# Attention scores on half the array: two heads on the partitions, three products of 64 rows per head

## The chip, the cores and the metric

The kernel runs on one core of a Trainium2 chip. The metric is the device time in microseconds of one execution. A profiled execution gives the trace; its span goes from the first to the last instruction, and the execution's own time is a little longer.

## What is computed

One decoder layer on 2048 tokens of width 1024. After a first RMSNorm the input is projected to u (512 columns), q (8 heads of 64), k and v (2 heads of 64 each). u goes through an S5 state-space branch with a GLU at its end; q, k and v go through attention in a sliding window of 128 with a sink per head. Both branches are normalised, joined, projected by w_out and added to the input; a SwiGLU layer follows. The part that the change touches:

```python
def one_block(args):                       # a block is 128 queries
    q_blk, k_blk, v_blk, blk = args        # k_blk, v_blk: the block before and this one, 256 keys
    valid = band & (blk * BLOCK - BLOCK + kj >= 0)
    s = jnp.einsum('bqhgd,bkhd->bhgqk', q_blk, k_blk).astype(jnp.float32) * scale
    s = jnp.where(valid, s, MASK_VALUE)
    m = jnp.maximum(jnp.max(s, axis=-1, keepdims=True), sink)
    p = jnp.exp(s - m)
    p = p / (jnp.sum(p, axis=-1, keepdims=True) + jnp.exp(sink - m))
    return jnp.einsum('bhgqk,bkhd->bqhgd', p.astype(v_blk.dtype), v_blk)
```

A head has 64 dimensions; four query heads share one key head.

## The kernel before

Precision comes from splitting: a float32 operand x is written as hi + lo, both of the type fp32r, which TensorE multiplies in one pass, and a product of two such operands is hi*hi + hi*lo + lo*hi (`mm3`, lines 219 to 221; the splits are lines 170 and 171, ScalarE for hi and VectorE for lo). Plain float32 operands take longer per column; the state-space products (`ps_S`, `ps_Y`), the transposes (`ps_pt`, `ps_oT`) and the attention outputs (`ps_O`) are of that kind.

The layer runs in stages: the projection to u; the projection to q, k, v woven with the state-space branch; the mixing stage; the SwiGLU layer, which takes more than half of the time. The mixing stage (`phase_mix`) weaves two generators. `dense_stream` does, for each of four blocks of 512 tokens, the GLU products (`ps_z`) and then the output projection (`ps_wo`), and `attn_stream` does attention in 16 tiles of 128 queries. `step` pulls the next step of the attention stream at high priority; first come `lead` = 6 steps, and then a number of steps per dense step that a rate sets (`lg`, `rate`). The program is not run in the order of the text: a planner puts each engine's instructions into an order by priority and by when their operands and buffers will be there, and inserts the waits. DMAs that are issued from one queue (SP's, mostly) are issued in order, so one that waits for a buffer holds up those behind it.

`attn_block` prepares a block of 512 tokens. k lies on the partitions twice, rows 0 to 63 and rows 64 to 127 with the same 64 dimensions (two loads, `kraw`), and is split into KH and KL. q is loaded in four pairs of heads, each pair twice as well, into rows 0 to 63 and into rows 64 to 127 (two loads of 256 KB per pair, line 797, buffers `qraw`, two of them, shared with `kraw`). For each head a tile QS of 128 rows is made: a copy to fp32r of all rows (line 800), and then in rows 64 to 127 the remainder (line 801, recorded as line 75, the helper `tt`). So QS holds q's hi in the upper half and q's lo in the lower half. Each of these five preparations ends in a `yield`.

`attn_tile` computes the scores of 128 queries with 256 keys. Per head there are two products over all 128 rows: QS with KH gives (hi + lo) * KH (line 820), and QS with KL adds (hi + lo) * KL (line 821). Two heads share a PSUM bank (`ps_sc`), so a tile fills four banks of eight, out of a group of four that the transposes and outputs of attention use as well (`bank`, tag "pa"). ScalarE copies a bank's first 128 keys to `prob` (line 826), and VectorE writes the second 128 over it where the mask allows (line 827). Maximum, exponential, transposes, outputs and the split of the result follow, each in a step of its own. `mx` and what comes after want all eight heads.

The state-space branch (`ssm_pair`) has the only products of the stage before that use half of the array: `ps_S` (line 658) has a stationary operand of 128 rows and 64 columns, one for each half of the output partitions.

Of the kernel before, what the change touches and what calls it, by code (L numbers as in the profile page):

```python
# [9 lines left out]
F32 = mybir.dt.float32  # L10
F32R = mybir.dt.float32r
# [3 lines left out]
ALU = mybir.AluOpType  # L15
# [4 lines left out]
P = 128  # L20
# [5 lines left out]
TB = SEQ // NB  # L26
# [7 lines left out]
MASKED = -1e30  # L34
# [9 lines left out]
def f32(ap):  # L44
    return ap.bitcast(F32)


class Layer:
# [730 lines left out]
    def attn_block(self, b, ready):  # L779
        nc, aw = self.nc, self.aw  # L780
        KH = aw.tile([P, 2, TB + P], F32R, tag="KH", name=f"KH_{b}")
        KL = aw.tile([P, 2, TB + P], F32R, tag="KL", name=f"KL_{b}")
        if b:
            for new, old in zip((KH, KL), self.kh_prev):
                nc.vector.tensor_copy(new[:, :, 0:P], f32(old[:, :, TB:TB + P]))
        self.kh_prev = (KH, KL)
        kraw = aw.tile([P, 2, TB], F32, tag="qraw", name=f"kraw_{b}", bufs=2)
        for o in (0, 64):
            nc.sync.dma_start(kraw[o:o + 64], self.k_d[b].rearrange("v r t -> r v t"))
        nc.scalar.copy(KH[:, :, P:], kraw)  # L790
        self.tt(KL[:, :, P:], kraw, f32(KH[:, :, P:]), ALU.subtract)
        yield
        QS = []
        for h in range(0, 8, 2):
            raw = aw.tile([P, 2, TB], F32, tag="qraw", name=f"qraw_{b}_{h}", bufs=2)
            for o in (0, 64):
                nc.sync.dma_start(raw[o:o + 64], self.q_d[b][h:h + 2].rearrange("h r t -> r h t"))
            for k in range(2):
                q = aw.tile([P, TB], F32R, tag="QS", name=f"QS_{b}_{h + k}", bufs=8)
                nc.scalar.copy(q, raw[:, k, :])  # L800
                self.tt(q[64:128], raw[64:128, k, :], f32(q[64:128]), ALU.subtract)
                QS.append(q)
            yield
        self.MA[b] = []
        ready[b] = (QS, KH, KL)

    def attn_tile(self, i, QS, KH, KL):

        nc, aw = self.nc, self.aw
        b, t = i // 4, i % 4  # L810
        tq = slice(t * P, (t + 1) * P)
        p = aw.tile([P, 8, P], F32, tag="prob", name=f"prob_{i}")
        for hp in range(4):
            sb = self.bank([P, 2, 2 * P], "sc")
            for h2 in range(2):
                h = hp * 2 + h2
                v = h // 4
                lo = P if i == 0 else 0
                ks = slice(t * P + lo, t * P + 2 * P)
                nc.tensor.matmul(sb[:, h2, lo:], QS[h][:, tq], KH[:, v, ks], start=True, stop=False)  # L820
                nc.tensor.matmul(sb[:, h2, lo:], QS[h][:, tq], KL[:, v, ks], start=False, stop=True)
            ph = p[:, hp * 2:hp * 2 + 2, :]
            if i == 0:
                nc.gpsimd.memset(ph, MASKED)
            else:
                nc.scalar.copy(ph, sb[:, :, 0:P])
            nc.vector.copy_predicated(ph, self.mask_qj.unsqueeze(1).to_broadcast([P, 2, P]), sb[:, :, P:])
        yield
        mx = self.tmp([P, 8], tag="mx")
        nc.vector.tensor_reduce(out=mx, in_=p, axis=AX.X, op=ALU.max)  # L830
        nm = self.tmp([P, 8], tag="nm")
        nc.vector.scalar_tensor_tensor(out=nm, in0=mx, scalar=self.rq[:, i:i + 1], in1=self.sinks,
                                       op0=ALU.mult, op1=ALU.max)
        es = self.tmp([P, 8], tag="es")
        self.tt(es, self.sinks, nm, ALU.subtract)
        nc.scalar.activation(es, es, AF.Exp)
        n = self.o1
        nc.vector.scalar_tensor_tensor(out=p[:, :n], in0=p[:, :n], scalar=self.rq[:, i:i + 1],
                                       in1=nm[:, :n].unsqueeze(2).to_broadcast([P, n, P]),
                                       op0=ALU.mult, op1=ALU.subtract)  # L840
        self.ts(nm[:, n:], nm[:, n:], -1.0, None, ALU.mult, ALU.bypass) if n < 8 else None
        for h in range(n, 8):
            nc.scalar.activation(p[:, h, :], p[:, h, :], AF.Exp, bias=nm[:, h:h + 1], scale=self.rq[:, i:i + 1])
        nc.scalar.activation(p[:, :n], p[:, :n], AF.Exp)
        yield
        if i:
            dv = aw.tile([P, 2, 65], F32, tag="dv", name=f"dv_{i}")
            self.tt(dv, self.V[:, i], self.V[:, i - 1], ALU.subtract, nc.gpsimd)
        else:
            dv = self.V[:, 0]  # L850
        pts = []
        for v in range(2):
            pt = self.bank([P, 4, P], "pt")
            for g in range(4):
                nc.tensor.transpose(pt[:, g, :], p[:, v * 4 + g, :], self.ident)
            pa = None
            if i:
                pa = aw.tile([P, 4, P], F32, tag="pa", name=f"pa_{i}_{v}")
                nc.scalar.copy(pa, pt)
            pc = aw.tile([P, 4, P], F32, tag="pc", name=f"pc_{i}_{v}")  # L860
            self.tt(pc, pa if i and self.o9 else pt, self.mask_jq.unsqueeze(1).to_broadcast([P, 4, P]), ALU.mult,
                    nc.gpsimd if i and self.o9 else None)
            pts.append((pc, pa))
        yield
        o = aw.tile([P, 8, 64], F32, tag="o", name=f"o_{i}")
        for v in range(2):
            O = self.bank([P, 4, 65], "O")
            for g in range(4):
                if i:
                    nc.tensor.matmul(O[:, g, :], pts[v][1][:, g, :], self.V[:, i - 1, v, :], start=True, stop=False)  # L870
                nc.tensor.matmul(O[:, g, :], pts[v][0][:, g, :], dv[:, v, :], start=(i == 0), stop=True)  # L871
            den = self.tmp([P, 4], tag="den")
            hs = slice(v * 4, v * 4 + 4)
            self.tt(den, O[:, :, 64], es[:, hs], ALU.add)
            nc.vector.reciprocal(den, den)
            self.tt(o[:, hs, :], O[:, :, 0:64], den.unsqueeze(2).to_broadcast([P, 4, 64]), ALU.mult)
        jk = aw.tile([P, 8, 64], BF16, tag="ojunk", name=f"ojunk_{i}", bufs=1)
        nc.scalar.activation(jk, o, AF.Square, accum_out=self.ssq_a[:, i:i + 1])
        yield
        oT = self.bank([P, 4, P], "oT")  # L880
        for c in range(4):
            nc.tensor.transpose(oT[:, c, :], o[:, 2 * c:2 * c + 2, :].rearrange("p h d -> p (h d)"), self.ident)
        mh = self.am.tile([P, 4, P], F32R, tag="mah", name=f"mah_{i}")
        ml = self.am.tile([P, 4, P], F32R, tag="mal", name=f"mal_{i}")
        self.split(mh, ml, oT)
        self.MA[b].append((mh, ml))
        yield
# [652 lines left out]
```

## Time and profile before

| | us |
|---|---|
| median of 3 runs | 2167.53 |
| lowest and highest | 2164.43 and 2172.02 |
| profiled execution, its own time | 2164.03 |
| its span | 2162.3 |
| TensorE busy (matmuls) | 2012.2 |
| VectorE busy | 1389.5 |
| ScalarE busy | 925.1 |
| TensorE's granted clock, mean | 0.975 |

In the views below PE is TensorE's matmuls, PEld its weight loads (which run beside the matmuls), DVE VectorE, ACT ScalarE, POOL GpSimd, SPq the DMA queue of SyncE. Times are us from the span's start unless marked ns. Matmuls are pipelined, so the recorded duration of one is longer than the distance to the next; what a matmul costs in a stream is the distance between starts. "128\*128" or "128\*64" is the part of the array in use, rows by columns. PEclk is the granted clock as a share of full speed.

### The profile page before, as it was taken

The page shows a single profiled execution, that of the slowest core. Times are in us where ns is not written, and L with a number is a line of the kernel's source. Part 1 is how long each engine was busy: PE and PEld are TensorE (multiplying, and loading weights), DVE is VectorE, ACT ScalarE, POOL GpSimd, SP SyncE. Part 2 cuts the span into 40 slices and gives each one's busy share as a digit, 9 for nine tenths or more (in the row PEclk, how much of TensorE's full clock was granted, in tenths as well). Part 3 has the DMA queues.
Part 4 walks back from the last instruction along what each step waited for, and adds up shares of the span by engine and source line. Part 5 has one row for each costly group of instructions (what it writes and reads, how often), then busy time and mean ns, then how long its engine had stood idle before and what let it go on. Part 6 is the DMA issues. An engine that isn't in the chain of part 4 may idle for free.

```text
span 2162.3 us, 25813 instructions
## 1 busy us (share of the span) xinstructions
PE 2012.2 (93%) x9200; PEld 1631.6 (75%) x9200; DVE 1389.5 (64%) x2199; ACT 925.1 (43%) x1468; POOL 301.7 (14%) x655
## 2 busy tenths in 40 slices
PE   7998887999999797999989998999999999999996
PEld 5777665787878675878768876887788888888885
DVE  7876888887676748556455655446766555554446
ACT  6433114976566545333323334345333333334443
POOL 3211000112223322212122110001100000000001
PEclk9999998999899998999999999999999999999998
DMA  8566657534246745657666476666523222246665
GB/s 276 213 229 191 200 148 190 144 100 158 67 148 202 270 155 178 240 138 204 208 194 155 153 264 218 199 192 231 171 102 124 95 99 105 89 165 224 204 195 185
DMA packets 177425, 379.73 MB, mean 176 GB/s; under 512 B 32864, under 2 KB 53856, under 8 KB 177104
## 3 DMA queue, kind: packets, MB, share of 16 engines
q1 hardware_dynamic: 138112, 259.89, 38.1%
q0 software_dynamic: 32512, 109.79, 15.6%
q10 hardware_dynamic: 6672, 8.40, 1.3%
q8 instruction: 72, 1.18, 0.2%
q14 instruction: 57, 0.47, 0.1%
HBM read 281.87 MB, written 119.21 MB: 185 GB/s over the span
## 4 chain that ended last, share of the span: by engine, by line
PE 42%; issue 27%; DMA 10%; DVE 7%; POOL 4%; ACT 3%; SPq 0%; DVEq 0%; POOLq 0%; ACTq 0%
PE ps_dn L221 5%; PE ps_dn L219 5%; PE ps_dn L220 5%; PE ps_gb L219 2%; PE ps_gb L221 2%; PE ps_gb L220 2%; PE ps_wo L219 2%; PE ps_wo L221 2%; PE ps_wo L220 2%; DMA hx<-hd 1%; DMA hr<-bTd 1%; DMA tab<-tabd 1%; PE ps_O L871 1%; PE ps_O L870 1%; PE ps_gc L219 1%
## 5 line engine op out<-in xcount | busy, mean ns | idle before, releaser
L219 PE MATMUL ps_gb<-bh,wh 128*128 128x512 f32 x704 | 280.3, 399 | 17.6 <-ACT wh L170 8.3
L221 PE MATMUL ps_gb<-bh,wl 128*128 128x512 f32 x704 | 275.8, 394 | 3.8 <-DVE wl L171 3.7
L220 PE MATMUL ps_gb<-bl,wh 128*128 128x512 f32 x704 | 277.7, 394 | 0.3 <-DVE bl L171 0.2
L221 PE MATMUL ps_dn<-wh_d,wl_x 128*128 128x512 f32 x616 | 241.4, 393 | 7.5 <-DVE wl_x L171 5.5
L219 PE MATMUL ps_dn<-wh_d,wh_x 128*128 128x512 f32 x616 | 241.3, 392 | 6.1 <-ACT wh_x L170 3.2
L220 PE MATMUL ps_dn<-wl_d,wh_x 128*128 128x512 f32 x616 | 240.7, 391 | 0.0
L219 PEld LDWEIGHTS ps_gb<-bh,wh 128*128 128x128 f32 x704 | 133.4, 190 | 54.3 <-ACT wh L170 10.4
L221 PEld LDWEIGHTS ps_gb<-bh,wl 128*128 128x128 f32 x704 | 133.4, 189 | 34.5 <-DVE wl L171 4.9
L220 PEld LDWEIGHTS ps_gb<-bl,wh 128*128 128x128 f32 x704 | 133.5, 190 | 29.8 <-DVE bl L171 1.5
L219 PE MATMUL ps_gc<-bh,wh 128*128 128x512 f32 x352 | 138.6, 396 | 6.9 <-ACT bh L170 6.7
L221 PEld LDWEIGHTS ps_dn<-wh_d,wl_x 128*128 128x128 f32 x616 | 115.8, 189 | 36.3 <-DVE wl_x L171 9.2
L170 ACT CAST wh<-fr 128x1024 fp32r<-128x1024 f32 (+1 forms) x88 | 73.4, 835 | 158.5 <-issue 87.4
L219 PEld LDWEIGHTS ps_dn<-wh_d,wh_x 128*128 128x128 f32 x616 | 116.3, 189 | 31.7 <-ACT wh_x L1089 4.2
L220 PE MATMUL ps_gc<-bl,wh 128*128 128x512 f32 x352 | 138.8, 395 | 0.0
L221 PE MATMUL ps_gc<-bh,wl 128*128 128x512 f32 x352 | 138.6, 394 | 0.0
L171 DVE TENSOR_TENSOR wl_x<-xr,wh_x 128x1024 fp32r<-128x1024 f32 x72 | 81.6, 1133 | 88.8 <-ACT wh_x L170 88.8
L171 DVE TENSOR_TENSOR wl_d<-dr,wh_d 128x1024 fp32r<-128x1024 f32 x84 | 95.1, 1132 | 61.5 <-ACT wh_d L170 61.5
L220 PEld LDWEIGHTS ps_dn<-wl_d,wh_x 128*128 128x128 f32 x616 | 116.3, 189 | 24.1
L170 ACT CAST wh_x<-xr 128x1024 fp32r<-128x1024 f32 x72 | 70.7, 982 | 118.9 <-PE ps_dn L220 115.6
L170 ACT CAST wh_d<-dr 128x1024 fp32r<-128x1024 f32 x84 | 82.4, 981 | 89.2 <-PE ps_dn L220 64.1
L75 DVE TENSOR_TENSOR q<-ps_ga,q 128x512 f32<-128x512 f32 x44 | 30.4, 690 | 113.7 <-PE ps_ga L221 113.2
L171 DVE TENSOR_TENSOR wl<-sb,wh 128x1024 fp32r<-128x1024 f32 x44 | 53.8, 1223 | 67.2 <-ACT wh L170 67.2
(368 smaller groups left out, 4623.1 us busy)
## 6 DMA issues: line engine op xcount, KB each, us to landing
fr<-in_w_gu SPq DMA_DIRECT2D x88, 512.0 KB
xr<-fxd SPq DMA_DIRECT2D x70, 512.0 KB
dr<-wsd SPq DMA_DIRECT2D x40, 512.0 KB
fxd<-f POOLq DMA_DIRECT2D x22, 768.0 KB, 4.3
gwr_o<-in_w_out SPq DMA_DIRECT2D x64, 256.0 KB
wsd<-in_w_down POOLq DMA_DIRECT2D x30, 512.0 KB, 10.6
dr<-in_w_down SPq DMA_DIRECT2D x30, 512.0 KB
raw<-in_xT SPq DMA_DIRECT2D x56, 256.0 KB
```

Of the source, the lines that this page charges most:

```text
L75: (eng or self.nc.vector).tensor_tensor(out=out, in0=a, in1=b, op=op)
L170: nc.scalar.copy(hi, x)
L171: nc.vector.tensor_tensor(out=lo, in0=x, in1=f32(hi), op=ALU.subtract)
L219: t.matmul(out, wh, mh, start=first, stop=False, skip_group_check=more)
L220: t.matmul(out, wh, ml, start=False, stop=False, skip_group_check=more)
L221: t.matmul(out, wl, mh, start=False, stop=last, skip_group_check=more)
L870: nc.tensor.matmul(O[:, g, :], pts[v][1][:, g, :], self.V[:, i - 1, v, :], start=True, stop=False)
L871: nc.tensor.matmul(O[:, g, :], pts[v][0][:, g, :], dv[:, v, :], start=(i == 0), stop=True)
```

## The change

q is loaded once, four heads at a time: of a pair of heads the even one lands on rows 0 to 63 and the odd one on rows 64 to 127. The load of four heads is one DMA of 512 KB. It is split into a tile qh and a tile ql, each [128, 2, 512], with one copy and one subtraction (`split`). The buffers QS become five of 4 KB per partition instead of eight of 2 KB. There are two `yield`s for q per block instead of four.

The scores of a head are now three products of 64 rows: qh with KH, qh with KL, ql with KH. For each group of four heads two banks are taken, one for the even heads (rows 0 to 63) and one for the odd heads (rows 64 to 127), and the products alternate between the two. The copies out of the banks write every second head of `prob`. The product lo * KL, which the old form contained, is not computed.

```diff
--- before.py
+++ after.py
@@ -791,15 +791,13 @@
         self.tt(KL[:, :, P:], kraw, f32(KH[:, :, P:]), ALU.subtract)
         yield
         QS = []
-        for h in range(0, 8, 2):
-            raw = aw.tile([P, 2, TB], F32, tag="qraw", name=f"qraw_{b}_{h}", bufs=2)
-            for o in (0, 64):
-                nc.sync.dma_start(raw[o:o + 64], self.q_d[b][h:h + 2].rearrange("h r t -> r h t"))
-            for k in range(2):
-                q = aw.tile([P, TB], F32R, tag="QS", name=f"QS_{b}_{h + k}", bufs=8)
-                nc.scalar.copy(q, raw[:, k, :])
-                self.tt(q[64:128], raw[64:128, k, :], f32(q[64:128]), ALU.subtract)
-                QS.append(q)
+        for v in range(2):
+            raw = aw.tile([P, 2, TB], F32, tag="qraw", name=f"qraw_{b}_{v}", bufs=2)
+            nc.sync.dma_start(raw, self.q_d[b][4 * v:4 * v + 4].rearrange("(p h) r t -> (h r) p t", h=2))
+            qh = aw.tile([P, 2, TB], F32R, tag="QS", name=f"QH_{b}_{v}", bufs=5)
+            ql = aw.tile([P, 2, TB], F32R, tag="QS", name=f"QL_{b}_{v}", bufs=5)
+            self.split(qh, ql, raw)
+            QS.append((qh, ql))
             yield
         self.MA[b] = []
         ready[b] = (QS, KH, KL)
@@ -810,21 +808,23 @@
         b, t = i // 4, i % 4
         tq = slice(t * P, (t + 1) * P)
         p = aw.tile([P, 8, P], F32, tag="prob", name=f"prob_{i}")
-        for hp in range(4):
-            sb = self.bank([P, 2, 2 * P], "sc")
-            for h2 in range(2):
-                h = hp * 2 + h2
-                v = h // 4
-                lo = P if i == 0 else 0
-                ks = slice(t * P + lo, t * P + 2 * P)
-                nc.tensor.matmul(sb[:, h2, lo:], QS[h][:, tq], KH[:, v, ks], start=True, stop=False)
-                nc.tensor.matmul(sb[:, h2, lo:], QS[h][:, tq], KL[:, v, ks], start=False, stop=True)
-            ph = p[:, hp * 2:hp * 2 + 2, :]
-            if i == 0:
-                nc.gpsimd.memset(ph, MASKED)
-            else:
-                nc.scalar.copy(ph, sb[:, :, 0:P])
-            nc.vector.copy_predicated(ph, self.mask_qj.unsqueeze(1).to_broadcast([P, 2, P]), sb[:, :, P:])
+        lo = P if i == 0 else 0
+        ks = slice(t * P + lo, t * P + 2 * P)
+        for v in range(2):
+            sb = [self.bank([P, 2, 2 * P], "sc") for _ in range(2)]
+            qh, ql = QS[v]
+            for pr in range(2):
+                for n, (q, k) in enumerate(((qh, KH), (qh, KL), (ql, KH))):
+                    for g in range(2):
+                        s = slice(g * 64, g * 64 + 64)
+                        nc.tensor.matmul(sb[g][:, pr, lo:], q[s, pr, tq], k[s, v, ks], start=n == 0, stop=n == 2)
+            for g in range(2):
+                ph = p[:, 4 * v + g:4 * v + 4:2, :]
+                if i == 0:
+                    nc.gpsimd.memset(ph, MASKED)
+                else:
+                    nc.scalar.copy(ph, sb[g][:, :, 0:P])
+                nc.vector.copy_predicated(ph, self.mask_qj.unsqueeze(1).to_broadcast([P, 2, P]), sb[g][:, :, P:])
         yield
         mx = self.tmp([P, 8], tag="mx")
         nc.vector.tensor_reduce(out=mx, in_=p, axis=AX.X, op=ALU.max)
```

## Rows read from the trace of the kernel before

**Rows 1.** The page, its first part: busy us, share of the span and instructions of three engines.

```profile
PE 2012.2 (93%) x9200; PEld 1631.6 (75%) x9200; DVE 1389.5 (64%) x2199; ACT 925.1 (43%) x1468; POOL 301.7 (14%) x655
```

**Rows 2.** The timeline of TensorE: the first score product, the first GLU product (the only score products between the two are those of the first head pair), and the first row of the last group of score products. Columns: start, busy us, engine, line, operation, out<-in, array, operand, count. From the first to the last there are 256 score products, which other TensorE work divides into 66 runs.

```profile
355.13 0.44 PE L820 MATMUL ps_sc<-KH,QS 128*128 128x128 f32 x1 [3.14 <-DVE QS L75]
...
356.88 2.07 PE L219 MATMUL ps_z<-yh,gwh_g 128*128 128x512 f32 x4 [0.54 <-ACT yh L170]
...
661.17 0.38 PE L820 MATMUL ps_sc<-KH,QS 128*128 128x256 f32 x1 [0.97 <-DVE prob L827]
```

**Rows 3.** Stretches of the stage: length; busy us and instructions of PE, PEld, DVE, ACT, POOL; granted clock; share of the DMA engines; GB/s.

```profile
344.00:700.00 356.00, 324.90 (x1827) 276.30 (x1826) 262.74 (x498) 244.44 (x472) 78.88 (x207) 0.95 0.48 140
...
340.00:360.00 20.00, 11.79 (x40) 8.58 (x39) 15.87 (x29) 8.04 (x15) 1.58 (x3) 0.70 0.65 170
...
540.00:560.00 20.00, 16.07 (x73) 14.97 (x73) 7.79 (x17) 6.34 (x14) 5.02 (x13) 0.66 0.33 96
```

**Rows 4.** Who made TensorE's matmuls wait between 336 and 720 us: us in total, times, longest.

```profile
PE ps_sc L820 <- DVE QS L75: 8.4, 7, 3.1
PE ps_wo L219 <- DVE mixr L997: 5.3, 2, 4.8
...
PE ps_sqs L985 <- POOL sqs L75: 4.2, 2, 3.9
PE ps_wo L219 <- DVE glu L954: 3.1, 2, 1.5
...
PE ps_wo L219 <- ACT sig L952: 1.8, 1, 1.8
```

**Rows 5.** Groups of instructions between 344 and 700 us, shapes kept apart (busy us, mean ns of one), and the q loads as the DMA queue issued them (ns of an issue: least, median, most; first and last start).

```profile
L820 PE MATMUL ps_sc<-KH,QS 128*128 128x256 f32 x120 | 35.7, 318 | 6.4 <-DVE QS L75 5.0 <-DVE prob L827 1.0 <-DVE o L75 0.3
L75 DVE TENSOR_TENSOR QS<-qraw,QS 64x512 fp32r<-64x512 f32 x32 | 21.7, 698 | 7.3 <-ACT QS L800 6.8
L800 ACT CAST QS<-qraw 128x512 fp32r<-128x512 f32 x32 | 18.8, 619 | 18.4 <-PE ps_sc L821 11.3 <-DMA qraw<-qd 7.0
L75 DVE TENSOR_TENSOR KL<-kraw,KH 128x1024 fp32r<-128x1024 f32 x4 | 5.0, 1258 | 0.0
L790 ACT CAST KH<-kraw 128x1024 fp32r<-128x1024 f32 x4 | 4.2, 1055 | 0.0
...
L797 SPq DMA_DIRECT2D qraw<-qd x32: 573/600/1123, 336.8 to 566.6; - x32
```

**Rows 6.** The timeline of the DMA queue SP at the start of the stage: a q load, the first load of the state-space result behind it, and the next q loads.

```profile
350.69 0.58 SPq L797 DMA_DIRECT2D qraw<-qd  x1
351.31 0.61 SPq L925 DMA_DIRECT2D yraw<-yTd  x1
355.62 1.88 SPq L797 DMA_DIRECT2D qraw<-qd  x3
```

**Rows 7.** The timeline of TensorE over the scores of the third tile (rows of one form in sequence are merged, with their count).

```profile
383.08 0.36 PE L820 MATMUL ps_sc<-KH,QS 128*128 128x256 f32 x1
...
383.63 0.28 PE L820 MATMUL ps_sc<-KH,QS 128*128 128x256 f32 x1
383.75 0.28 PE L821 MATMUL ps_sc<-KL,QS 128*128 128x256 f32 x1
383.87 0.33 PE L871 MATMUL ps_O<-Vres,pc 128*128 128x65 f32 x2
384.01 0.36 PE L820 MATMUL ps_sc<-KH,QS 128*128 128x256 f32 x1
384.21 0.33 PE L871 MATMUL ps_O<-Vres,pc 128*128 128x65 f32 x2
384.35 0.36 PE L821 MATMUL ps_sc<-KL,QS 128*128 128x256 f32 x1
...
384.69 0.36 PE L820 MATMUL ps_sc<-KH,QS 128*128 128x256 f32 x1
...
385.93 0.28 PE L820 MATMUL ps_sc<-KH,QS 128*128 128x256 f32 x1
...
387.51 0.37 PE L821 MATMUL ps_sc<-KL,QS 128*128 128x256 f32 x1
```

**Rows 8.** The timeline of TensorE around one group of ps_S, the products that use half of the columns, and then two answers for the 0.03 us from 333.19 to 333.22 alone: the weight loads and the matmuls that start there.

```profile
332.24 0.59 PE L685 MATMUL ps_Y<-U,tab 128*128 128x256 f32 x2
332.67 0.59 PE L686 MATMUL ps_Y<-X,tab 128*128 128x256 f32 x2
333.20 1.08 PE L658 MATMUL ps_S<-U,tab 128*64 128x256 f32 x8
334.21 0.70 PE L685 MATMUL ps_Y<-U,tab 128*128 128x256 f32 x2
334.75 0.60 PE L636 MATMUL ps_vt<-ident,qe 128*128 128x128 f32 x4
...
333.20 0.14 PEld L658 LDWEIGHTS ps_S<-U,tab 128*64 128x64 f32 x2 [0.33 <-PE ps_Y L685]
...
333.20 0.44 PE L658 MATMUL ps_S<-U,tab 128*64 128x256 f32 x2
```

**Rows 9.** The timeline of TensorE inside one group of attention outputs: the third and the eleventh of its rows, two products each.

```profile
389.55 0.39 PE L870 MATMUL ps_O<-Vres,pa 128*128 128x65 f32 x2
...
391.34 0.39 PE L870 MATMUL ps_O<-Vres,pa 128*128 128x65 f32 x2
```

## The prediction, made before the changed kernel was run

> **What bounds the kernel now.** I read the page's busy shares first: TensorE is busy for 93% of the span, VectorE for 64%, ScalarE for 43% [rows 1]. The change touches only the attention scores, so next I looked for the stage that holds them. The first score product starts at 355 us and the last group at 661 us [rows 2], inside the stage that mixes attention with the GLU and output projections. The stretch 344 to 700 us stands for it: TensorE is busy for 324.9 of 356 us, VectorE for 262.7, ScalarE for 244.4 [rows 3]. So TensorE bounds this stage too, with 31.1 us in which it is idle. The waits that I can name are small and scattered: scores for q splits 8.4 us, output projection for mixr 5.3, the row sums for POOL 4.2, GLU hand-overs 3.1 and 1.8, together 22.8 [rows 4]. Two stretches are worse than the rest: 340 to 360 us, where the state-space part runs out and TensorE's granted clock is 0.70, and 540 to 560 us with 0.66 [rows 3], a mix of its two levels (1.2 and 2.4 GHz). So TensorE work added in this stage mostly reaches the end, and ScalarE or VectorE work taken out mostly does not.
>
> **The change part by part.**
>
> *Loads.* 32 issues of 256 KB on SP [rows 5] become 8 of 512 KB: each q byte is read once, not twice, 4.2 MB instead of 8.4. The stage uses 0.48 of the DMA engines [rows 3], so this is worth something only where SP or a landing is late. At the start SP stands still until the k split frees a raw buffer, issues q at 350.69 and, behind it, the first y load at 351.31 [rows 6]; the y load leads to the first GLU product. In the new order the second q load waits for the same k split with y behind it again, so I take 0. The trace does not show the new order. Its bounds: a gain of 5 us (SP no longer waits at 355.62 for three more q issues [rows 6]), a loss of 2 (512 KB land later).
>
> *Splits.* ScalarE: 32 casts of 619 ns, 19.8 us, become 8 of the k form, 1055 ns, 8.4 us: 11.4 us less. VectorE: 32 subtractions of 698 ns, 22.3 us, become 8 of 1258 ns, 10.1 us: 12.2 us less [rows 5]. Both engines have slack, so only waits that end on them count: 8.4 us of TensorE waiting for q [rows 4]. About 3 us of that lies before 355.1 us, where the first GLU product is not ready anyway (it starts at 356.88 [rows 2]). I count 3.5 us as gained, with 0 and 8.4 as bounds. A first split is now longer (1.06 + 1.26 instead of 0.62 + 0.70 us) but there are two per block, not eight.
>
> *Products.* Before: two per head, 16 per tile, 256 in all; one is issued every 0.12 us (383.63, 383.75, 383.87 [rows 7]), half of what a 512-column product takes. At 0.118 us for 240 of them (120 in each of the two forms [rows 5]) and 0.11 for the 16 of the first tile this is 30.1 us. After: 24 per tile, 384 in all, each on 64 rows. The price hangs on whether the two heads of a pair run at the same time. No 64-row product is in this trace, but there are products that use half the array the other way: ps_S, 64 columns wide. Two S loads and two S matmuls start within 0.03 us, and eight S matmuls take 1.01 us (333.20 to 334.21), where eight full-width ones at the spacing of Y (0.43 us for two) would take 1.72 [rows 8]. So halves do run in pairs, loads included. By this nearest row the scores need 192 pair slots of 0.118, 22.6 us: 7.5 less than now. The other bound: if halves cannot load weights at the same time, each product pays a load of 128 columns. The O products move only 65 columns and still come two in 0.22 us (389.55 to 391.34, 16 in 1.79), 0.111 each [rows 9], so the load sets that spacing; 384 of those are 42.6 us, 12.5 more than now. I take the pairs, from the S rows. The Trainium skill (TensorE: Matmul & The Clock Gate, LDWEIGHTS) has a load's time follow its columns, not its rows; an estimate from its formula is 107 ns for 128 columns, which the O spacing agrees with, and by that alone halving the rows saves nothing in the load.
>
> *Entering and leaving the half-array mode.* This is the term against the change. From Y to S the spacing is 0.53 us instead of 0.43 (+0.10); the S group takes 1.01 instead of four slots of 0.215, 0.86 (+0.15, its first load and its drain); the two Y that follow take 0.54 instead of 0.43 (+0.11, a load that could not run ahead) [rows 8]. That is 0.36 us per visit with loads of 64 columns; with 128 columns the entering load costs 0.05 more: 0.41 us. A score visit costs nothing of the kind today: O, one score, O take 0.14 + 0.20 us, what the parts take alone [rows 7]. The Trainium skill (TensorEngine Tiling (Array Packing), Key Properties) says that a change of tiling mode drains the engine; the trace agrees, 0.53 against 0.43 us, though for columns, and by a free switch the sum would be 7.5 us lower than now on TensorE, not higher.
>
> How many visits? Counted from the first to the last group of score products there are 66 runs now [rows 2]. Third-tile scores alone fall into six: 383.08, 384.01, 384.35, 384.69, 385.93 and 387.51 us, with O pairs, GLU products and transposes between them [rows 7]. The cause is an order planned by readiness, with four PSUM banks shared by scores, transposes and O. After, two banks are filled together by 12 products, which makes 32 groups at least if each is unbroken. I take 50, between 32 and 66: 20.5 us (bounds 13.1 and 27.1). Broken groups also lose some pairs: I count 6.4 of the 7.5 us.
>
> *Evictions, softmax, order.* The copies and masked copies keep their count and size and only address heads in steps of two: 0. A bank is given back after 12 products instead of 4, which makes ScalarE's copy start later; TensorE has other work then: 0, the masked copy's wait of at most some tenths if not. The attention stream has two steps fewer per block, so attention stands two steps earlier in the order against the projections. It may move any of the waits of [rows 4]: 0, with 5 us either way.
>
> *Sum.* TensorE: +20.5 - 6.4 = +14.1 us. Of these 91% (324.9 of 356) meet a busy engine: +12.8. Less 3.5 for the splits: +9.3. Profiled execution: 2164.0 us (span 2162.3, 1.7 around it), so 2173.3. The median of the runs shown is 2167.5, 3.5 above it; on that scale 2177, 0.4% slower. A measurement of this kernel tells about 0.3% (6.5 us) from no change.
>
> **The rivals.**
>
> *The switch is nearly free, or groups stay whole, and it is faster.* The trace shows the drain for column halves only. If row halves change over without it, TensorE does 7.5 us less and the scores wait less for q: 7.5 x 0.91 + 3.5 = 10.3 us, 2157. The turning point is 7.5 us over the visits: 0.15 us each at 50 visits. For it: S loads and matmuls overlap almost perfectly. Against it: all three surcharges stand in the rows, and the entry and exit are not hidden. 0.25.
>
> *No change that can be told.* Few visits (about 32: 13.1 - 7.5 = 5.6 us of TensorE), part of them beginning where TensorE was idle anyway (31.1 us of idle time), and the splits give it back: between -6 and +6, 2167. For it: the change is small against the span. 0.28.
>
> *Halves do not pair.* Loads go one after another: +12.5 us instead of -6.4, with 20.5 for the visits 33.0, x 0.91 - 3.5 = +26.5: 2194. For it: S loads have 64 columns and leave room in a slot of 0.215 us; two score loads of 0.111 do not fit into one slot of 0.118 unless they truly run together. Against it: two S loads start within 0.03 us. 0.12.
>
> *The forecast* has 0.35, its own range from 32 to 66 visits 2170 to 2185.
>
> **How the numbers follow.** Slower: 0.35 + 0.12 = 0.47. Same: 0.28. Faster: 0.25. The range leaves out the outer half of the rival that doesn't pair and the outer third of the faster one: 2155 to 2196.
>
> **What would show it.** Right: score matmuls in twos a few hundredths apart, a pair every 0.12 us; about 0.3 us to the first product after a visit and a long first load there; 40 to 66 visits; ScalarE's q casts at 8.4 us and VectorE's at 10.1; TensorE's busy time in the stage nearly the same but the stage some 10 us longer. Wrong: a pair every 0.22 us or more (no pairing), O or projection products directly behind a score at 0.12 us (no drain), well over 66 visits (then slower than forecast), or a stage that moves by its waits, the one at 540 to 560 us above all, and not by its scores.

## The result

The changed kernel takes 2193.8 us (median of 5 runs, 2191.3 to 2210.7) against 2167.5 us: a ratio of 1.0129 with a 95% interval of 1.0101 to 1.0157, so it is slower, by 26 us. Its profiled execution took 2193.8 us, with a span of 2192.0. The page's first part, to be read beside [rows 1]:

```profile
PE 2046.2 (93%) x9328; PEld 1647.1 (75%) x9328; DVE 1379.1 (63%) x2175; ACT 918.9 (42%) x1445; POOL 298.4 (14%) x655
```

TensorE is busy 34 us longer; VectorE and ScalarE do 10 and 6 us less. Most of the difference lies in the mixing stage. From here on the stage is measured in every kernel from the start of the last Y product to the start of the first product of the SwiGLU layer (`ps_gb`), so that what happens before and after it does not count. First the kernel before, then the changed one; columns as in [rows 3].

```profile
351.36:802.05 450.69, 410.44 (x2195) 344.71 (x2194) 321.75 (x570) 288.75 (x537) 110.19 (x275) 0.95 0.52 159
```

```profile
353.32:826.87 473.55, 439.07 (x2323) 356.25 (x2322) 311.19 (x547) 281.76 (x513) 106.96 (x275) 0.94 0.45 142
```

The stage is 22.9 us longer (473.55 against 450.69), and 28.6 us of TensorE time are added in it. Of the 29.7 us between the two spans another 2.0 lie ahead of the stage and 4.9 behind it, where the work is the same. The groups that answer to [rows 5], between 344 and 700 us:

```profile
L820 PE MATMUL ps_sc<-KH,QH 64*128 64x256 f32 x120 | 36.3, 360 | 1.0 <-DVE prob L827 0.4 <-DVE o L75 0.3
L171 DVE TENSOR_TENSOR QL<-qraw,QH 128x1024 fp32r<-128x1024 f32 x8 | 9.7, 1216 | 3.2 <-PE ps_sc L820 3.0
L170 ACT CAST QH<-qraw 128x1024 fp32r<-128x1024 f32 x8 | 8.4, 1051 | 0.3 <-DMA qraw<-qd 0.3
```

The splits came out as they were costed: 8.4 us on ScalarE and 9.7 on VectorE, for 19.8 and 22.3 before. The wait for q is nearly gone: where [rows 4] has 8.4 us, the changed kernel has 1.9 between 336 and 720 us.

```profile
PE ps_pt L855 <- DVE prob L827: 2.4, 2, 2.0
...
PE ps_sc L820 <- ACT QH L170: 1.9, 1, 1.9
```

Its score products have three more waits of 0.3 to 0.4 us. The first line is a new wait: transposes wait for the masked copies that give a bank back.

So the loss is to be looked for in the products. A visit is a run of score products with no other product of TensorE between them; a pair is two score products that start within 0.055 us. There are two main kinds of visit in the timeline of TensorE. This is one as it was meant, twelve products in pairs:

```profile
386.44 0.39 PE L870 MATMUL ps_O<-Vres,pa 128*128 128x65 f32 x2
386.76 0.40 PE L820 MATMUL ps_sc<-KH,QH 64*128 64x256 f32 x2
386.98 0.29 PE L820 MATMUL ps_sc<-KL,QH 64*128 64x256 f32 x2
387.10 0.29 PE L820 MATMUL ps_sc<-KH,QL 64*128 64x256 f32 x2
...
387.46 0.28 PE L820 MATMUL ps_sc<-KH,QL 64*128 64x256 f32 x2
387.67 0.44 PE L871 MATMUL ps_O<-dv,pc 128*128 128x65 f32 x2
```

Two products start together (the count is 2 in each row) and inside the visit a pair follows every 0.12 us. The two of a pair start 0.005 to 0.016 us apart here. And this is the commoner one (22 of the 59 visits have six products), between output projections:

```profile
433.25 0.48 PE L221 MATMUL ps_wo<-gwh_o,mal 128*128 128x512 f32 x1
433.57 0.40 PE L219 MATMUL ps_wo<-gwh_o,mah 128*128 128x512 f32 x1
433.90 0.38 PE L820 MATMUL ps_sc<-KH,QH 64*128 64x256 f32 x1
434.12 0.28 PE L820 MATMUL ps_sc<-KL,QH 64*128 64x256 f32 x1
434.24 0.28 PE L820 MATMUL ps_sc<-KH,QL 64*128 64x256 f32 x1
...
434.60 0.28 PE L820 MATMUL ps_sc<-KH,QL 64*128 64x256 f32 x1
434.80 0.50 PE L220 MATMUL ps_wo<-gwl_o,mah 128*128 128x512 f32 x1
435.14 0.39 PE L219 MATMUL ps_wo<-gwh_o,mah 128*128 128x512 f32 x1
```

Six products of one half, one after the other at the same 0.12 us; the other half's six come in a visit of their own. In the whole trace 59 visits hold 82 pairs of 192 possible ones; 74 of the pairs start within 0.02 us, the rest within 0.05. The edges of the visit show its price. From the projection to the first score product 0.33 us pass instead of 0.23 (433.57 to 433.90), from the first to the second 0.22 instead of 0.12, from the last to the projection 0.20 instead of 0.12, and from that to the next 0.34 instead of 0.23: together 0.40 us. Behind an O product, where 27 of the visits stand, it is 0.34 us: a round of one score product and two O products takes 0.68 us there instead of 0.34 (its rows are under e9).

### The profile page after: what moved, and what is told of

It reads as the page before. It is cut to its first block, busy times and chain, and to the rows that moved or that the text cites. A ratio compares the mean times of both kernels' runs of the same rounds, so it can differ in the third digit from the quotient of the medians.

```text
span 2192.0 us, 25983 instructions
## 1 busy us (share of the span) xinstructions
PE 2046.2 (93%) x9328; PEld 1647.1 (75%) x9328; DVE 1379.1 (63%) x2175; ACT 918.9 (42%) x1445; POOL 298.4 (14%) x655
## 4 chain that ended last, share of the span: by engine, by line
PE 60%; issue 11%; DMA 10%; DVE 7%; POOL 3%; ACT 2%; SPq 0%; DVEq 0%; POOLq 0%; ACTq 0%
PE ps_gb L219 6%; PE ps_gb L221 5%; PE ps_gb L220 5%; PE ps_dn L221 5%; PE ps_dn L220 5%; PE ps_dn L219 5%; PE ps_gc L219 3%; PE ps_gc L221 3%; PE ps_gc L220 3%; PE ps_sc L820 2%; PE ps_wo L219 2%; PE ps_wo L220 2%; PE ps_wo L221 2%; PE ps_O L871 1%; PE ps_ga L221 1%
## 5 line engine op out<-in xcount | busy, mean ns | idle before, releaser
L219 PEld LDWEIGHTS ps_gb<-bh,wh 128*128 128x128 f32 x704 | 134.1, 191 | 56.8 <-ACT f L1285 11.8
```

Of the source, the lines that this page charges most:

```text
L219: t.matmul(out, wh, mh, start=first, stop=False, skip_group_check=more)
```

## The experiments

All times are ratios to runs of the kernel before on the same chip. "Stage" is the stretch defined above, in the profiled execution; visits and pairs are counted in its trace.

| kernel | ratio, 95% interval | stage, us | visits | pairs |
|---|---|---|---|---|
| before | 1 | 450.7 | none (66 runs on the full array) | |
| changed | 1.0129, 1.0101 to 1.0157 | 473.6 | 59 | 82 |
| e1, products in the order of the text | 1.0041, 1.0018 to 1.0065 | 460.0 | 64 | 155 |
| e2, same order, full array | 1.0020, 1.0004 to 1.0036 | 449.7 | none | |
| e3, 192 products, full array | 0.9915, 0.9893 to 0.9937 | 437.7 | none | |
| e4, before with q loaded once | 1.0007, 0.9989 to 1.0026 | 447.9 | none | |
| e5, changed, four steps ahead | 1.0125, 1.0080 to 1.0169 | 477.5 | 73 | 87 |
| e6, whole groups | 0.9993, 0.9969 to 1.0016 | 449.8 | 43 | 163 |
| e7, whole tiles | 1.0079, 1.0053 to 1.0104 | 460.9 | 23 | 189 |
| e8, before with half of q's preparation | 0.9996, 0.9972 to 1.0019 | 443.3 | none | |
| e9, changed, one half of the array only | 1.0183, 1.0140 to 1.0225 | 495.0 | 59 | 0 |
| e11, changed again | 1.0138, 1.0084 to 1.0192 | 474.0 | 59 | 80 |
| e12, whole groups first | 0.9955, 0.9936 to 0.9974 | 436.6 | 27 | 187 |
| e13, before, products first | 1.0011, 0.9989 to 1.0033 | 452.8 | none | |

**e1: is it the order that loses the pairs?**

```diff
-    nc.tensor.matmul(sb[g][:, pr, lo:], q[s, pr, tq], k[s, v, ks], ...)
+    ins = nc.tensor.matmul(sb[g][:, pr, lo:], q[s, pr, tq], k[s, v, ks], ...)
+    if pr or n or g:
+        self.tc.keep_in_program_order(ins)
```

> The twelve score products of a bank pair are tied to one another in the order of the text, so that even and odd head alternate; nothing else is changed. In the changed kernel 82 of 192 possible pairs ran together (counted in its trace). Theory (the gain is lost because the planned order fills one bank and then the other, so that halves do not meet): about 186 pairs, 104 x 0.118 = 12 us less on TensorE, about as many visits as before (59 to 64), so 2180 to 2186 us. Rival (pairs are there but the stage is bound by something else, or pairs cost as much as two products): 2190 to 2197 us.

Measured: 1.0041, 0.9% or 19 us better than the changed kernel, and the stage 13.6 us shorter, with five visits more. The theory holds: the pairs were lost in the planned order. But 73 pairs more and five visits more account for only 6.6 of the 13.6 us. Added up over stretches of 10 us, TensorE spends 41 us of this stage at the lower clock and 60 in the changed kernel's, which is worth some 9 us (how much of that time is lost stands under e2). Only 155 of the forecast 186 pairs came about, because the first product of a group often goes ahead alone, as soon as the first of its two banks is free, and the other eleven follow in a visit of their own.

**e2: what does the mode cost?**

```diff
-    s = slice(g * 64, g * 64 + 64)
-    nc.tensor.matmul(sb[g][:, pr, lo:], q[s, pr, tq], k[s, v, ks], ...)
+    nc.tensor.matmul(sb[g][:, pr, lo:], q[:, pr, tq], k[:, v, ks], ...)
```

> The same 384 score products in the same planned order, but over all 128 rows, so the array is never divided: the two heads of a pair are not kept apart (each score is the sum of two heads'), nothing else is left out. Theory (a visit to the half-array mode costs about 0.4 us, 59 visits): the switches go, -23 us on TensorE, the 82 pairs go too, +9.7 us: 2178 to 2184 us. Rival (switching is nearly free, the loss is the 128 more products alone and the later start of the stage): +9 us, 2200 to 2205 us.

Measured: 1.0020, 24 us better than the changed kernel, though it has no pairs. The visits are the same, with the same numbers of score products between the same other products, so the 23.9 us that the stage is shorter (473.55 to 449.66) are put down to the mode: what 59 visits cost, less what 82 pairs save, and what the clock does. It was more than the theory said (13 us):

```profile
360.98:810.64 449.66, 416.90 (x2322) 355.12 (x2321) 309.08 (x546) 280.88 (x513) 109.57 (x275) 0.96 0.48 150
```

The granted clock in the stage is 0.96, in the changed kernel 0.94. Added up over stretches of 10 us, with levels of 1.2 and 2.4 GHz, that is 34 us at the lower level against 60. At that level the changed kernel's score products come every 0.21 us instead of 0.12 (402.19, 402.40) and the GLU products of the kernel before every 0.43 instead of 0.23 (359.47, 359.90, 360.32), so a little less than half of the time is lost: some 12 of the 26 us. With 32 visits at 0.40 us and 27 at 0.34, 22.0 - 82 x 0.118 + 12 = 24.3 us, against the 23.9 of one execution of each kernel; the agreement is no better than a few us. Where the clock falls is the subject of e9.

**e3: what would free pairs be worth?** (half of the products, on the full array)

```diff
-    for n, (q, k) in enumerate(((qh, KH), (qh, KL), (ql, KH))):
-        for g in range(2):
+    for g in range(2):
+        two = ((qh, KH), (qh, KL))[:2 - (pr + g) % 2]
+        for n, (q, k) in enumerate(two):
```

> 192 full-array score products instead of 384 (half of the products are left out and the two heads of a pair are not kept apart), which is the TensorE time that perfect pairs would have if the mode cost nothing; loads, splits and copies are those of the changed kernel. Theory (loads and splits bring next to nothing, TensorE's work counts): 64 products fewer than before, -7.5 us against the kernel before: 2156 to 2164 us. Rival (the new loads, splits and the two steps fewer disturb the order and cost by themselves, as the first GLU product that comes 6.8 us later suggests): 2166 to 2175 us.

Measured: 0.9915, 18.5 us faster than before, more than either expected. Beside e2, 192 products fewer make 1.05% or 22.8 us less, 0.119 us each, as if TensorE's work in this stage reached the end in full. The two profiled executions do not bear that out. Of the 27.4 us between their spans only 11.9 lie in the stage, where e3 has 45 us at the lower clock against 34, which takes some 5 us back; 10.5 us lie ahead of the stage, where the work is the same. So the share is more than half; that it is all of it is not shown. What e3 does show is that the new loads, splits and steps do not cost time by themselves.

**e4 and e8: q's loads and splits alone.** In e4 the products of the kernel before stay, and q is loaded once per pair of heads:

```diff
-    for o in (0, 64):
-        nc.sync.dma_start(raw[o:o + 64], self.q_d[b][h:h + 2].rearrange("h r t -> r h t"))
-    for k in range(2):
-        q = aw.tile([P, TB], F32R, ...)
-        nc.scalar.copy(q, raw[:, k, :])
-        self.tt(q[64:128], raw[64:128, k, :], f32(q[64:128]), ALU.subtract)
...
+    nc.sync.dma_start(raw[0:64], self.q_d[b][h:h + 2].rearrange("h r t -> r h t"))
+    q = aw.tile([P, 2, TB], F32R, ...)
+    nc.scalar.copy(q[0:64], raw[0:64])
+    self.tt(q[64:128], raw[0:64], f32(q[0:64]), ALU.subtract)
...
```

> The kernel before with one part of the change: q is loaded once per pair of heads, into rows 0 to 63 alone, and split with one copy and one subtraction per pair, which writes the remainder into rows 64 to 127; the products stay 128 rows, two per head. Theory (the loads are off the path, the splits nearly): 2162 to 2169 us, no change that can be told. Rival (q's loads and splits are on the path): 2155 to 2161 us.

Measured: 1.0007, no change that can be told. In e8 half of q's preparation is left out altogether:

```diff
-    for h in range(0, 8, 2):
+    for h in range(0, 4, 2):
...
-    ready[b] = (QS, KH, KL)
+    ready[b] = (QS + QS, KH, KL)
```

> The kernel before, with only four of the eight heads' q loaded and split per block and used twice (so the scores of heads 4 to 7 are those of heads 0 to 3; that part is left out), which takes half of q's loads and splits away as the change does: ScalarE 9.9 and VectorE 11.1 us less. The products stay as they are. Theory (the splits stood on the path by TensorE's wait of 8.4 us for q, and the changed kernel's other parts therefore cost more than its total shows): ratio to the kernel before 0.994 to 0.997. Rival (the splits are hidden, the 3.5 us of the prediction or less): 0.998 to 1.001.

Measured: 0.9996. The rival holds: the splits are hidden, or worth so little that these runs cannot tell it. In its profiled execution the stage is 7 us shorter all the same, and the SwiGLU layer longer by as much, so one execution is not enough to tell; the time decides.

**e5: does the later start of the GLU products cost?** In the changed kernel the first GLU product starts at 363.6 us instead of 356.9 [rows 2], because 48 score products stand ahead of it.

```diff
-    self.lead = 6
+    self.lead = 4
```

> The changed kernel with four attention steps instead of six before the first GLU product, so that only one tile's scores (not two) stand ahead of it, as in the kernel before. The planned order then has 73 visits instead of 59 and about as many pairs. Theory (what counts is visits and pairs; the later start of the GLU products only exchanges one work for another): 14 visits more, about +6 us against the changed kernel, ratio to the kernel before 1.012 to 1.018. Rival (the later start is part of the loss): 4 to 7 us less than the changed kernel in spite of the visits, 1.008 to 1.011.

Measured: 1.0125, with 73 visits. The interval, 1.0080 to 1.0169, holds both answers; the stage is 3.9 us longer than the changed kernel's, which is nearer to the theory. It settles little.

**e9 and e11: pairs, and where the clock falls.** In e9 both heads use the same half, so the mode and the order stay and no two products can run together:

```diff
-    s = slice(g * 64, g * 64 + 64)
+    s = slice(0, 64)
```

> The changed kernel in its planned order, with both heads of a pair on rows 0 to 63 (the odd head's scores are the even head's; its own are left out): half-array mode as before, 59 visits, but no two products can run together. Theory (82 pairs save 0.118 us each): the stretch from the last Y product to the first ps_gb product, 473.5 us in the changed kernel, becomes about 483, ratio to the kernel before 1.015 to 1.020; and the granted clock falls to half again near 400 and 500 us, where single score products stand between pairs of O products, while TensorE is busy (10 us lost in the changed kernel, none in the same order on the full array). Rival (pairs bring nothing in this order, or the clock falls by chance): 470 to 476 us, 1.010 to 1.014, the clock falling elsewhere or not at all.

> The changed kernel as it is, beside the run with one half on the same chip. Theory: ratio to the kernel before 1.010 to 1.015, and the clock falls to half in the same two places (near 400 and near 500 us after the span's start, shifted with the start of the stage). Rival: the same ratio, but the clock falls elsewhere, so that the drop has nothing to do with the single score products.

Measured: e9 1.0183, e11 1.0138. The stage of e9:

```profile
360.59:855.54 494.95, 462.83 (x2323) 380.38 (x2322) 310.27 (x546) 282.10 (x513) 107.10 (x275) 0.91 0.43 136
```

It is 21.4 us longer than the changed kernel's, 12 more than the theory said, as the pairs alone make 82 x 0.118 = 9.7. The clock is 0.91 in it, 92 us at the lower level against 60, some 14 us of lost work; with the pairs that is 24, a little more than the difference. So pairs do bring time, which is as much as this can tell, and the clock is low for longer when they are missing. It falls in the same two places, and beside them in some that differ from one execution to the next (e11 has a fall at 497.2 us that the changed kernel's first trace lacks). In the changed kernel near 400 and 500 us, in stretches of 2 us:

```profile
400.00:402.00 2.00, 2.00 (x12) 1.62 (x11) 1.30 (x3) 1.03 (x3) 0.59 (x1) 0.58 0.50 194
...
498.00:500.00 2.00, 2.00 (x11) 1.49 (x10) 1.28 (x5) 1.76 (x5) 0.00 (x0) 0.83 0.08 4
500.00:502.00 2.00, 2.00 (x7) 1.43 (x6) 0.00 (x0) 0.41 (x2) 0.00 (x0) 0.50 0.34 127
502.00:504.00 2.00, 2.00 (x10) 1.54 (x9) 0.16 (x1) 0.00 (x0) 0.41 (x1) 0.50 0.00 0
```

TensorE is busy throughout (2.00 us of 2.00), and nothing keeps it waiting; what surrounds the second fall is this, a score product alone, or once one of each half, between pairs of O products:

```profile
498.33 0.38 PE L820 MATMUL ps_sc<-KH,QH 64*128 64x256 f32 x1
498.33 0.38 PE L820 MATMUL ps_sc<-KL,QH 64*128 64x256 f32 x1
498.64 0.44 PE L871 MATMUL ps_O<-dv,pc 128*128 128x65 f32 x2
499.01 0.38 PE L820 MATMUL ps_sc<-KL,QH 64*128 64x256 f32 x1
499.32 0.69 PE L870 MATMUL ps_O<-Vres,pa 128*128 128x65 f32 x2
499.94 0.58 PE L820 MATMUL ps_sc<-KH,QL 64*128 64x256 f32 x1
500.45 0.69 PE L871 MATMUL ps_O<-dv,pc 128*128 128x65 f32 x2
501.07 0.58 PE L820 MATMUL ps_sc<-KH,QL 64*128 64x256 f32 x1
```

Each round of one score and two O products takes 0.68 us (498.33 to 499.01) and, at the lower clock, 1.13 (499.94 to 501.07); its work is 0.34. In e2 the same round is:

```profile
496.03 0.36 PE L819 MATMUL ps_sc<-KL,QH 128*128 128x256 f32 x1
496.23 0.33 PE L869 MATMUL ps_O<-Vres,pa 128*128 128x65 f32 x2
496.36 0.36 PE L819 MATMUL ps_sc<-KH,QL 128*128 128x256 f32 x1
496.56 0.33 PE L870 MATMUL ps_O<-dv,pc 128*128 128x65 f32 x2
496.71 0.36 PE L819 MATMUL ps_sc<-KH,QL 128*128 128x256 f32 x1
```

0.34 us, and the clock stays at full speed:

```profile
496.00:498.00 2.00, 2.00 (x20) 2.00 (x19) 1.14 (x4) 2.00 (x5) 0.34 (x1) 1.00 0.20 19
498.00:500.00 2.00, 2.00 (x14) 1.78 (x14) 1.97 (x5) 1.55 (x5) 0.08 (x1) 1.00 0.32 112
```

In e11 such visits start at 404.66 to 407.14 us and 506.44 to 509.82, and the clock falls at 408.5 and 510.9; in e9 at 408.51 to 410.99 and 519.85 to 523.36, with the fall at 412.0 and 524.6. Three executions with the mode fall at the same two places of the order, and e2, which has the same order without the mode, at neither. Other orders agree: in e1 single products stand at 419.31 to 422.70 and 491.63 to 494.33 us, with falls at 422.6 and 494.3, and e12, below, has no visit of fewer than twelve products and no fall through 300 us of the stage. It does not happen each time: e6 has five such visits in a row (484.46 to 487.16 us) and stays at full speed. The rows of e12 and of e6:

```profile
368.50:668.80 300.30, 285.34 (x1802) 235.12 (x1802) 224.19 (x458) 216.53 (x417) 73.12 (x200) 1.00 0.39 120
```

```profile
484.00:488.00 4.00, 4.00 (x22) 2.95 (x22) 0.46 (x2) 1.48 (x4) 0.01 (x1) 1.00 0.43 135
```

So the fall goes with rows of single visits, and what decides whether one comes was not isolated.

**e6 and e7: fewer visits.** The first product of a group is planned only when the group's other bank is free too; a write of one column claims it.

```diff
+    both = nc.vector.memset(sb[1][:, 0, lo:lo + 1], 0.0)
...
     if pr or n or g:
         self.tc.keep_in_program_order(ins)
+    else:
+        self.tc.add_manual_dep(ins.ins, both.ins.name, ...)
```

> As the run with the products in the order of the text, and the first product of a group is planned only when the group's second bank is free too (VectorE writes one column of it before; 32 tiny writes more). The order has 43 visits instead of 64, and all but a few pairs are whole. Theory (each visit costs 0.4 to 0.5 us, the pairs the rest): 21 visits x 0.45 = 9.5 us and some 30 pairs x 0.118 = 3.5 us less than that run: ratio to the kernel before 0.996 to 1.000. Rival (the loss lies with the pairs alone, visits are mostly covered): 1.002 to 1.006.

Measured: 0.9993, as the theory had it: 21 visits fewer than e1 and 8 pairs more, 9.3 us by their prices, go with 10.2 us of stage. In e7 the same is done for the four banks of a tile (`SB`, four banks taken at once, three of them written to, and all 24 products in one order):

> The same for the 24 products of a tile and its four banks (48 tiny writes more): 23 visits, all pairs whole. Theory: 41 visits x 0.45 = 18.5 us and 3.5 us of pairs less than the run with the products in the order of the text: ratio to the kernel before 0.991 to 0.996, faster than before. Rival (to wait for four free banks holds up transposes and outputs, which share them, and TensorE runs dry): 0.999 to 1.010.

Measured: 1.0079. Here the theory fails and the rival holds. There are 23 visits and 189 pairs, and TensorE is busy 9 us less than in e6 (406.8 against 416.0), but it stands idle for 54 us of the stage instead of 34. Transposes now wait for the copies out of the banks that all belong to the scores; the kernel before has no such wait in that window. From the waits of e7 between 340 and 812 us:

```profile
PE ps_pt L863 <- DVE prob L835: 7.9, 11, 3.7
...
PE ps_oT L890 <- DVE pc L75: 4.4, 1, 4.4
```

**e12 and e13: a version that beats both.** e6, with its score products at a higher priority than the O products, so that none of these comes between:

```diff
+    with self.tc.high_priority(200):
         for pr in range(2):
             for n, (q, k) in enumerate(((qh, KH), (qh, KL), (ql, KH))):
...
```

> The run with whole groups, whose score products now also have a higher priority than the attention outputs, so that none of these comes between them: 27 visits instead of 43, every pair whole. Computes all of it. Theory (0.4 us per visit, pairs, and less time at half clock): 16 x 0.4 = 6.4 us and some 25 pairs x 0.118 = 3 us less than the run with whole groups (0.9993): ratio to the kernel before 0.992 to 0.998. Rival (outputs that come later hold up what follows and eat the gain, as with whole tiles): 0.999 to 1.006.

> The kernel before, with the same higher priority for its score products and nothing else: 51 runs of score products instead of 66, on the full array. It shows whether the priority helps by itself. Theory (a visit costs nothing on the full array): ratio 0.998 to 1.002. Rival (the order helps whatever the mode): 0.992 to 0.997.

Measured: e12 0.9955, as the theory had it, its whole interval below 1: 2160.5 us against 2171.0 on the same chip. The kernel before with the same priority: 1.0011. The stage of e12 and one of its visits, between projections:

```profile
354.48:791.05 436.57, 403.51 (x2323) 329.50 (x2322) 308.85 (x577) 279.58 (x513) 111.18 (x275) 0.96 0.49 154
```

```profile
437.65 0.40 PE L220 MATMUL ps_wo<-gwl_o,mah 128*128 128x512 f32 x1
437.98 0.38 PE L822 MATMUL ps_sc<-KH,QH 64*128 64x256 f32 x2
438.20 0.28 PE L822 MATMUL ps_sc<-KL,QH 64*128 64x256 f32 x2
...
438.68 0.28 PE L822 MATMUL ps_sc<-KH,QL 64*128 64x256 f32 x2
438.89 0.50 PE L221 MATMUL ps_wo<-gwh_o,mal 128*128 128x512 f32 x1
439.23 0.39 PE L219 MATMUL ps_wo<-gwh_o,mah 128*128 128x512 f32 x1
```

The edges cost the same 0.40 us (0.33, 0.22, 0.21 and 0.34 us stand where 0.23, 0.12, 0.12 and 0.23 would), but there are 27 of them, and the score rows have the count 2. The clock is 0.96 as on the full array. TensorE's busy time in the stage is 403.5 us, 7 less than before.

## Why the prediction was right, and what was missed

The direction and the mechanism were right, and the time lies in the range: entering and leaving the half-array mode outweighs what pairs save, and q's cheaper preparation does not make up for it. The size was not: 9.3 us were forecast and 26 came, outside the forecast's own range of 2170 to 2185. That 2193.8 still lies within 2155 to 2196 is luck: the upper end was there for the rival in which halves do not pair, at 2194 us, and halves do pair. One of the prediction's own signs failed too: TensorE's busy time in the stage was to stay nearly the same, and it grew by 28.6 us. Step by step:

- **Pairing.** That halves run in pairs, loads included, read from the ps_S products of [rows 8], was right: mostly within 0.02 us, a pair every 0.12 us. The size of the term was wrong. "Broken groups also lose some pairs: I count 6.4 of the 7.5 us" stands for some 183 pairs; there were 82. 128 more products at 0.118 us, less 82 pairs, are +5.4 us instead of -6.4, 11.8 us off. The prediction had the cause in hand, an order planned by readiness with four shared banks [rows 7], and used it for the count of visits but not for the alternation inside a group: a bank that comes free alone gets all its products at once.
- **Price of a visit.** 0.41 us forecast from [rows 8]; 0.40 measured between projections and 0.34 behind O products. Columns told the price of rows well.
- **Count of visits.** 50 forecast, 59 came: 22.0 us at these prices instead of 20.5.
- **The clock.** Not in the sum at all. 60 us of the stage lie at the lower level, 44 in the kernel before: some 7 us of lost work; against e2's order it is 12.
- **91% of TensorE's added work.** By the times of e2 and e3 it would be all of it (22.8 us for 192 products of 0.118); by their stages it is less, as said under e3. The 91% is neither confirmed nor refuted.
- **Splits.** 3.5 us were counted. The wait for q did shrink by 6.5 us in the trace, but e4 and e8 show no time in it. They tell 0.2%, some 4 to 5 us, so the 3.5 us are not refuted. What takes the place of that wait was not isolated.
- **Loads, evictions, softmax.** Nothing was counted. For the loads e4 shows nothing. For the evictions the prediction allowed some tenths; transposes waited 2.4 us for masked copies. No run isolates that or the softmax.

The terms do not close fully. 5.4 + 22.0 + 7 less 6.5 for the wait for q make 27.9 us, and the stage grew by 22.9; e2, with 128 products more than the kernel before (15.1 us), is only 4 us slower. For e2 the traces say where most of it went: TensorE is idle for 33 us of its stage instead of 40 (449.66 less 416.90, 450.69 less 410.44), and 34 us lie at the lower clock instead of 44. Why the new order does that no run isolates, and the 5 us of the changed kernel stay open.

## What to carry to other kernels

Products on half of the array pay only in company: both halves' products must stand next to each other in the queue, and many of them per visit, since each visit costs 0.34 to 0.40 us here, about three full products of 256 columns. When an order is planned by readiness, two products that are meant to run together have to be tied together, with both of their banks claimed first, and kept from being interleaved; with the same 384 products the kernel took between 0.9955 and 1.0138 of the time of the kernel before, depending on their order (the ties cost 32 one-column writes, and the priority by itself brought nothing, e13). Tying too much costs as well: with four banks claimed at once the waits took the gain back (e7). Counting a mechanism from a neighbouring one in the trace (columns for rows) was sound; what has to be asked as well is whether the planner will leave it alone.

## What was not expected of the hardware

TensorE's granted clock fell to 0.50, its lower level, while the engine was recorded as busy without a gap, behind a few single half-array products that stood between O products, each with its entry and exit: in all three executions of that order with the mode, in e1's order too, and not in the same order without the mode (1.00 through the same products). It is no certain consequence, as e6 shows. The fall costs more than the mode: a round that takes 0.34 us on the full array takes 0.68 with the mode and 1.13 after the fall.

The Trainium skill (TensorE: Matmul & The Clock Gate, A second HAM failure mode: psum-queue depth-cycling) describes a kernel in which short idle times of TensorE between groups of matmuls make its clock swing between the two levels. The swing is here too, 1.00 to 0.50 at 400 and 500 us; the idle times are not in the records (2.00 us busy of 2.00). Since busy ends are modelled, the drains at the edges of each visit may be such idle times. That is argued, not shown: no run here changed the drains without changing the mode.
